# Places of a recurrence in the projections' memory, a memory projection in matmuls of 512 columns, and a preparation of two heads on one engine

## The chip, the cores and the metric

The kernel runs on one core of a Trainium2 chip. The metric is the device time of one execution in microseconds. The core has a matrix engine (TensorE, "PE" in the profile, with its weight loads as "PEld"), a vector engine (VectorE, "DVE"), a scalar engine (ScalarE, "ACT"), GpSimd ("POOL") and SyncE ("SP"), which in this kernel issues all DMAs. Each engine works through its own instructions in order and waits on semaphores for the others. Matmul results land in PSUM, eight banks of 128 rows by 512 fp32 values; all else lies in SBUF, 128 partitions wide.

## The reference, cut to what matters

One encoder layer on two sequences, 512 tokens (`x_sample`) and 256 tokens (`x_prompt`), 768 tokens in all, model width 1024. It has three parts: a mixer (an RWKV-7 recurrence beside a gated linear attention), a cross-attention to a memory of 256 rows per sequence, and a feed-forward layer.

```python
def rwkv7_scan(r, w, k, v, kk, a):
    def step(S, inp):
        r_t, w_t, k_t, v_t, kk_t, a_t = inp
        sa = jnp.einsum('bhij,bhj->bhi', S, -kk_t)
        S = (S * w_t[:, :, None, :] + sa[..., None] * (kk_t * a_t)[:, :, None, :]
             + v_t[..., None] * k_t[:, :, None, :])
        return S, jnp.einsum('bhij,bhj->bhi', S, r_t)
...
def hybrid_mixer(h, p):
    proj = h @ p['w_in']
    rw = centred_shift(proj[..., :R_COLS], p['mu_prev'], p['mu_next'])
    gl = proj[..., R_COLS:]
    mixed = jnp.concatenate([rwkv7_group(rw, p), gla_group(gl, p)], axis=-1)
    return mixed @ p['w_out']
...
def cross_attention(h, m, p):
    q = (h @ p['wq_x']).reshape(B, S, X_HEADS, X_HD)
    kv = (m @ p['wkv_x']).reshape(B, M, 2, X_HEADS, X_HD)
...
def encoder_trunk(x, mem, params):
        x = x + rms_norm(hybrid_mixer(rms_norm(x, p['g_mix_pre']), p), p['g_mix_post'])
        m = rms_norm(mem, p['g_mem'])
        x = x + rms_norm(cross_attention(rms_norm(x, p['g_x_pre']), m, p), p['g_x_post'])
        h = rms_norm(x, p['g_ffn_pre'])
        x = x + rms_norm(jnp.square(jax.nn.relu(h @ p['w_ff1'])) @ p['w_ff2'], p['g_ffn_post'])
```

The recurrence has 8 heads of 64 and runs once forwards and once backwards over each sequence. The gated linear attention (GLA) has 4 heads and is computed in chunks of 64 tokens, also in both directions.

## The kernel before, in words

All large products are split into a high and a low part (`split`, L143) and summed from three matmuls (`mm3`, L241). Weights are loaded as `wraw`, rounded by ScalarE to `whi` (L147), and the rest `wlo` is taken by GpSimd or VectorE (L148).

*Projections.* `hT_hi` and `hT_lo`, the normed input with its channels on the partitions, lie in pool `hp` on the right side of SBUF. Each block of 128 output channels is 24 matmuls of 512 columns and 24 of 256 (`channels_product`, L250). `gla_dense` (L468) makes the 16 blocks of the GLA and `rkv_early` (L446) the r, k, v blocks of a pair of heads; both write to DRAM through two tiles tagged `gd`. They are called through `blocks`, whose index is a GLA operand below 4 and a pair plus 3 from there on, so `(6, i)` are the three blocks of pair 3.

*Preparation of a pair* (`prep`, L692). The 8 heads of the recurrence are four pairs p, each with one head on partitions 0 to 63 and one on 64 to 127. For each direction d, `decays` makes the running product of decays, `bk_of` (L660) and `ar_of` (L669) form four products of 768 columns for each head, and `lower` (L678) makes the triangular part of 12 chunks of 64 tokens. In `bk_of` and `ar_of` VectorE works on the first head and GpSimd on the second, whose two operands lie in the opposite order. `invert` (L764) inverts the diagonal blocks of 32 by elimination on VectorE (L744, L746), and `joined` (L768) merges two blocks of 32 into one of 64 on TensorE (L788, L800). `begin` is `prep` plus a bonus term.

*The recurrence.* The chunks of a pair in both directions are grouped into 6 places g, each of 2560 columns. `products` (L973) loads a place's operands by six DMAs and computes what the steps use: 16 matmuls on 64 rows (L989 to L992) and 8 transposes (L1000). `step` (L1007) is one step of the recurrence: four groups of small matmuls (L1018, L1031, L1038, L1049) with ScalarE and VectorE in between. `stage(q)` (L1134) takes four steps, each for the second half of pair q-1 and the first and third part of pair q; there are stages 0 to 4. The places 0, 4, 1, 5, 2 lie in pool `mq1`, place 3 in `mq2`. The output of a pair goes to one of three tiles `ya`. `finish` (L1066) norms and gates it through a work tile `fb`.

*GLA heads.* `gla_head` (L825) works in an arena of 13 slots in pool `gp`: four slots alternate between even and odd heads, slots 8 to 12 are used by every head. Since `mq1` is opened when `gp` is closed, it lies on the arena's memory: no place can be loaded before the last head is done.

*Memory blocks.* `memory` (L1089) loads the two normed memories, 8 slices of 512 columns (256 for each sequence), into `mq2`, and `memory_block` (L1097) makes 16 blocks of keys and values from them, with 48 matmuls of 256 columns each (L1104). They stand between the steps of stages 1 to 3.

*Order.* A planner of the framework puts the instructions into the engines' queues. It takes them by a priority that is their order in the program, moved ahead by `high_priority(offset=...)` (steps by 4000, products by 3000, preparation and inversion by 2000 instructions), and by the times that its own model of the chip gives. A pool or a tag is reused when all that used the earlier tile is done. The program's order around the recurrence is: heads 0 to 3, preparations 1 and 2 and the blocks of L935 to L947; then products of pair 0, blocks `(6, i)`, stage 0, products for places 2 and 3, the loads of the memories, preparation 3, the join of pair 2, inversion 3, 16 memory blocks, stage 1, and so on. Behind the recurrence `w_out` is loaded into 32 planes of 512 columns, 20 of them on the places 0, 4, 1 and 5, and `out_projection` (L1251) follows, whose output `hh`, `hl` lies in a new pool on the right side.

Of the kernel before, what the change touches and what calls it, by code (L numbers as in the profile page):

```python
# [8 lines left out]
F32 = mybir.dt.float32  # L9
# [7 lines left out]
P = 128  # L17
D = 1024
# [14 lines left out]
def kernel(ctx: ExitStack, tc: tile.TileContext, I, y_prompt, y_sample):  # L33
# [30 lines left out]
    hp = hp_cm.__enter__()  # L64
    wp_cm = tc.tile_pool(name="wp", bufs=2, reuse_waits="tile")
# [380 lines left out]
    def rkv_early(p, i):  # L446

        ot = hp.tile([P, T], F32, tag="gd", bufs=2, name="gd")
# [8 lines left out]
    def tokens_first(ot):  # L457

        vt = hp.tile([P, T], F32, tag="gd", bufs=2, name="gd")
# [8 lines left out]
    def gla_dense(g, i):  # L468
# [3 lines left out]
        ot = hp.tile([P, T], F32, tag="gd", bufs=2, name="gd")  # L472
# [133 lines left out]
    tts, tdz = [], []  # L606
    for d in range(2):
        t = mp.tile([P, NCH, 64], F32, tag=f"tt{d}", name=f"tt{d}")
        pool.memset(t, 0.0)
        tts.append(t)  # L610
        tdz.append(mp.tile([P, NCH, 32], F32, name=f"tdz{d}"))
# [48 lines left out]
    def bk_of(pinv, nka, kd):  # L660

        b_ = pair_tile()
        dve.tensor_tensor(out=b_[0:64, :, 0, :], in0=v3(nka, 0, 64), in1=v3(pinv, 0, 64), op=ALU.mult)
        pool.tensor_tensor(out=b_[64:128, :, 1, :], in0=v3(nka, 64), in1=v3(pinv, 64), op=ALU.mult)
        dve.tensor_tensor(out=b_[0:64, :, 1, :], in0=v3(kd, 0, 64), in1=v3(pinv, 0, 64), op=ALU.mult)
        pool.tensor_tensor(out=b_[64:128, :, 0, :], in0=v3(kd, 64), in1=v3(pinv, 64), op=ALU.mult)
        return b_

    def ar_of(st, d):  # L669

        a_, kk, r_ = pair_tile(), st["kk"], st["r"]
        dve.tensor_tensor(out=a_[0:64, :, 0, :], in0=v3(kk, 0, 64), in1=px_prev[d][0:64], op=ALU.mult)
        pool.tensor_tensor(out=a_[64:128, :, 1, :], in0=v3(kk, 64), in1=px_prev[d][64:128], op=ALU.mult)
        pool.tensor_tensor(out=a_[64:128, :, 0, :], in0=v3(r_, 64), in1=px_at[64:128], op=ALU.mult)
        dve.tensor_tensor(out=a_[0:64, :, 1, :], in0=v3(r_, 0, 64), in1=px_at[0:64], op=ALU.mult)
        return a_

    def lower(st, d, b_, a_):  # L678

        lt = mp.tile([P, NCH, 64], F32, tag="lsb", bufs=4, name="lsb")  # L680
        for c0, n in ((0, 8), (8, 4)):
            pm = psn("low").rearrange("p (c x) -> p c x", x=64)
            for c in range(n):
                for h, hs in enumerate(HS):
                    pe.matmul(out=pm[hs, c, :], lhsT=b_[hs, c0 + c, h, :], rhs=a_[hs, c0 + c, h, :],
# [131 lines left out]
    with tc.tile_pool(name="gp", bufs=1, reuse_waits="tile") as gp:  # L817
# [134 lines left out]
    def open_places(pool_, gs):  # L952
        for g in gs:
            t = pool_.tile([P, 2560], F32, tag=f"pl{g}", name=f"pl{g}")
# [788 lines left out]
```

## Time and profile before

| | us |
|---|---|
| median of 3 runs | 1591.46 |
| lowest and highest of them | 1590.47, 1599.93 |
| the profiled execution | 1596.87 |
| its span, first to last instruction | 1595.0 |

The profile lists instructions with their line, engine, tiles and shapes. In a table of windows each row is a stretch of the span (start:end, length), then the busy time and the number of instructions of each engine, the TensorE clock that was granted (1.00 is full speed), the share of the DMA engines' time and the GB/s moved. In a timeline the columns are the start, the duration, engine, line, operation, tiles and shape, and in brackets the idle time before it and what ended that. In a list by line "x8: a/b/c" are the number of instructions and their shortest, median and longest duration in nanoseconds. Matmuls are pipelined: the distance between the starts of two says how long one holds the engine, its own duration says more than that.

Lines such as L247 or L148 belong to helpers that many parts of the kernel call; the tile names (`pd`, `wlo`, `bk`, `arena`) tell these parts apart.

### The profile page before, as it was taken

The numbers are of one execution on the slowest core, as the hardware profiler recorded it, in microseconds if no ns is written. First come the engines' busy times: TensorE is split into PE (matmuls) and PEld (weight loads), VectorE is DVE, ScalarE is ACT, GpSimd is POOL, SyncE is SP. The second block draws the span as 40 slices with busy tenths as digits, with TensorE's granted clock in tenths as the row PEclk, the third lists the DMA queues.
The fourth block names the chain that finished last, engine by engine and source line by source line (L and its number), as shares of the span: only waits on it lengthen the run. The fifth ranks groups of instructions, "written<-read, shape, count | busy, mean of one in ns | idle before, by whom it ended". The sixth has DMA issues, their size and how long they took to land. (4 is left out here: it accounts for less than half of the span.)

```text
span 1595.0 us, 28271 instructions
## 1 busy us (share of the span) xinstructions
PE 1442.8 (90%) x10614; PEld 1246.0 (78%) x10614; DVE 1049.7 (66%) x1605; ACT 718.9 (45%) x1417; POOL 514.6 (32%) x576
## 2 busy tenths in 40 slices
PE   7999689889887889899888999996999999999996
PEld 6887578777775777778767888786999999787785
DVE  5545885497577795764455434448876676878886
ACT  5754344443333332333344354434555556544442
POOL 6416643494317342211531354420000001231223
PEclk9999798989875988888979999997999999999998
DMA  6686555556468447754452333235555447564434
GB/s 168 181 302 188 167 137 131 145 146 192 111 205 229 127 149 176 205 134 135 126 166 99 119 95 105 73 111 160 172 169 176 158 145 284 171 204 132 143 100 142
DMA packets 279565, 250.35 MB, mean 157 GB/s; under 512 B 89264, under 2 KB 227059, under 8 KB 279428
## 3 DMA queue, kind: packets, MB, share of 16 engines
q1 hardware_dynamic: 279428, 248.54, 52.1%
q8 instruction: 84, 1.38, 0.4%
q14 instruction: 53, 0.43, 0.1%
HBM read 164.11 MB, written 82.58 MB: 155 GB/s over the span
## 5 line engine op out<-in xcount | busy, mean ns | idle before, releaser
L148 POOL TENSOR_TENSOR wlo<-wraw,whi 128x256 fp32r<-128x256 f32 x192 | 176.8, 934 | 331.0 <-ACT whi L147 231.1
L247 PE MATMUL pd<-hT_hi,whi 128*128 128x256 f32 (+1 forms) x512 | 182.0, 356 | 12.6 <-DVE gd L325 8.2
L247 PE MATMUL pd<-hT_hi,wlo 128*128 128x512 f32 (+1 forms) x512 | 180.1, 354 | 4.0 <-POOL wlo L148 4.0
L247 PE MATMUL pd<-hT_lo,whi 128*128 128x256 f32 (+1 forms) x512 | 178.6, 350 | 0.3 <-DVE hT_lo L206 0.3
L1511 POOL TENSOR_TENSOR wl<-w,wh 128x1024 fp32r<-128x1024 f32 x8 | 21.2, 2649 | 329.8 <-ACT wh L1510 329.8
L247 PEld LDWEIGHTS pd<-hT_hi,whi 128*128 128x128 f32 x512 | 100.4, 196 | 27.6 <-issue 5.5
L247 PEld LDWEIGHTS pd<-hT_hi,wlo 128*128 128x128 f32 x512 | 99.6, 195 | 18.6 <-POOL wlo L148 5.3
L147 ACT ACTIVATE whi<-wraw 128x256 fp32r<-128x256 f32 x192 | 77.3, 414 | 78.2 <-PE pd L1104 22.9
L247 PEld LDWEIGHTS pd<-hT_lo,whi 128*128 128x128 f32 x512 | 100.4, 196 | 13.0 <-DVE hT_lo L206 0.5
L148 DVE TENSOR_TENSOR ul<-ur,uh 128x768 fp32r<-128x768 f32 x56 | 77.4, 1388 | 30.7 <-ACT uh L147 17.7
L147 ACT ACTIVATE uh<-ur 128x768 fp32r<-128x768 f32 x56 | 47.4, 847 | 107.8 <-PE gz L1520 52.0
L1510 ACT ACTIVATE wh<-w 128x1024 fp32r<-128x1024 f32 x64 | 67.1, 1053 | 35.9 <-PE fz L1520 24.2
L1520 PE MATMUL gx<-wh,uh 128*128 128x512 f32 x192 | 75.0, 397 | 4.3 <-DVE acc L1713 4.3
L1511 DVE TENSOR_TENSOR wl<-w,wh 128x1024 fp32r<-128x1024 f32 x56 | 68.2, 1219 | 15.1 <-ACT wh L1510 14.5
L1520 PE MATMUL gx<-wl,uh 128*128 128x512 f32 x192 | 75.9, 395 | 0.0
L1520 PE MATMUL gx<-wh,ul 128*128 128x512 f32 x192 | 75.4, 395 | 0.0
L1520 PE MATMUL fz<-hh,wh 128*128 128x384 f32 x192 | 66.0, 344 | 1.9 <-ACT wh L1510 1.9
L1511 POOL TENSOR_TENSOR wl<-ws,wh 128x1024 fp32r<-128x1024 f32 x16 | 40.6, 2536 | 79.6 <-ACT wh L1510 79.6
L1520 PE MATMUL fz<-hh,wl 128*128 128x384 f32 x192 | 65.2, 344 | 0.8 <-DVE wl L1511 0.8
L1520 PE MATMUL fz<-hl,wh 128*128 128x384 f32 x192 | 65.8, 343 | 0.0
L1510 ACT ACTIVATE wh<-ws 128x1024 fp32r<-128x1024 f32 x48 | 50.5, 1052 | 26.8 <-PE fx L1520 22.3
L1104 PE MATMUL pd<-mem_hi,whi 128*128 128x256 f32 x256 | 59.3, 308 | 1.4 <-ACT mo L1116 1.4
(476 smaller groups left out, 4306.9 us busy)
## 6 DMA issues: line engine op xcount, KB each, us to landing
w<-in_w_ff_dram SPq DMA_DIRECT2D x64, 512.0 KB
ur<-ud SPq DMA_DIRECT2D x56, 384.0 KB
wraw<-in_w_in_dram SPq DMA_DIRECT2D x108, 128.0 KB
ud<-u SPq DMA_DIRECT2D x32, 384.0 KB
ud<-us SPq DMA_DIRECT2D x24, 384.0 KB
wraw<-in_wkv_x_dram SPq DMA_DIRECT2D x64, 128.0 KB
lora<-lo_t SPq DMA_DIRECT2D x20, 384.0 KB
bkg<-bkd SPq DMA_DIRECT2D x24, 256.0 KB
```

Of the source, the lines that this page charges most:

```text
L147: act.activation(out=hi, in_=src, func=AF.Copy)
L148: (lo_eng or pool).tensor_tensor(out=lo, in0=src, in1=hi, op=ALU.subtract)
L247: pe.matmul(out=out, lhsT=a, rhs=b, start=(i == 0), stop=(i == n - 1))
L1104: prev = order_after(pe.matmul(out=pd[:, c0:c0 + 256], lhsT=x, rhs=y[:, c0:c0 + 256], start=(k + i + c0 == 0), stop=(k + i + c0 == KD + 25 ...
L1510: act.activation(out=hi, in_=t[name], func=AF.Copy)
L1511: lo_eng.tensor_tensor(out=lo, in0=t[name], in1=hi, op=ALU.subtract)
L1520: pe.matmul(out=out, lhsT=a, rhs=b, start=first and i == 0, stop=last and i == n - 1, skip_group_check=True)
```

## The change

The places 0, 4, 1, 5 and 3 move into the memory of `hT_hi` and `hT_lo` (tags `hh` and `hl` of pool `hp`, which stays open), except for a part of place 3 that lies in `mq1` together with place 2. The tiles `gd` get a pool of their own, `gdp`; two of the tiles `ya` reuse them, the third reuses `kds`. `mq1` is opened on the right side. The pool `gp` of the GLA heads is closed later: heads 2 and 3, preparation 2 and inversion 2 now stand behind stage 0 and the products of places 2 and 3; the blocks `(6, i)` stand in front of them. `mq2`, with the memories, is opened after that. `finish` works in tag `sxf`, a tile of the inversions. 18 of the planes of `w_out` lie in a pool `wo1` that is opened on the left side.

A memory block is 24 matmuls of 512 columns, both memories at once. In `bk_of` and `ar_of` VectorE makes all four products on 128 partitions, with both heads in the same order; `products` turns the second head's order round where it loads the operands (two DMAs where one was) and where it transposes them (a transpose and a matmul with the identity where a transpose was).

```diff
@@ bk_of, ar_of, lower @@
-        dve.tensor_tensor(out=b_[0:64, :, 0, :], in0=v3(nka, 0, 64), in1=v3(pinv, 0, 64), op=ALU.mult)
-        pool.tensor_tensor(out=b_[64:128, :, 1, :], in0=v3(nka, 64), in1=v3(pinv, 64), op=ALU.mult)
-        dve.tensor_tensor(out=b_[0:64, :, 1, :], in0=v3(kd, 0, 64), in1=v3(pinv, 0, 64), op=ALU.mult)
-        pool.tensor_tensor(out=b_[64:128, :, 0, :], in0=v3(kd, 64), in1=v3(pinv, 64), op=ALU.mult)
+        dve.tensor_tensor(out=b_[:, :, 0, :], in0=v3(nka), in1=v3(pinv), op=ALU.mult)
+        dve.tensor_tensor(out=b_[:, :, 1, :], in0=v3(kd), in1=v3(pinv), op=ALU.mult)
...
+        dve.tensor_tensor(out=a_[:, :, 0, :], in0=v3(kk), in1=px_prev[d], op=ALU.mult)
+        dve.tensor_tensor(out=a_[:, :, 1, :], in0=v3(r_), in1=px_at, op=ALU.mult)
...
-                    pe.matmul(out=pm[hs, c, :], lhsT=b_[hs, c0 + c, h, :], rhs=a_[hs, c0 + c, h, :],
+                    pe.matmul(out=pm[hs, c, :], lhsT=b_[hs, c0 + c, 0, :], rhs=a_[hs, c0 + c, 0, :],
@@ order ahead of the recurrence @@
         blocks([(5, i) for i in range(3)])
-        gla_head(2)
         blocks([(3, 3), (2, 3)])
-        begin(2)
-        invert(2)
-        gla_head(3)
+        blocks([(6, i) for i in range(3)])
@@ places @@
-    mq1_cm = tc.tile_pool(name="mq1", bufs=1, reuse_waits="tile")
+    mq1_cm = tc.tile_pool(name="mq1", bufs=1, side="right", reuse_waits="tile")
     mq1 = mq1_cm.__enter__()
-    open_places(mq1, (0, 4, 1, 5, 2))
-    yas = [mq1.tile([P, T], F32, tag="ya0", name="ya0")]
+    plh, pll = (hp.tile([P, KD * T], F32, tag=n, name="pl_" + n) for n in ("hh", "hl"))
+    for t, gs in ((plh, (0, 4)), (pll, (1, 5))):
+        for i, g in enumerate(gs):
+            whole_place(g, t[:, 2560 * i:2560 * i + 2560])
+    place(3, plh[:, 5120:5632], pll[:, 5120:5888], mq1.tile([P, 512], F32, tag="pl3", name="pl3"), plh[:, 5632:6144],
+          pll[:, 5888:6144])
+    whole_place(2, mq1.tile([P, 2560], F32, tag="pl2", name="pl2"))
+    yas = [gdp.tile([P, T], F32, tag="gd", bufs=2, name=f"ya{i}") for i in range(2)]
@@ products @@
-        for h, hs in enumerate(HS):
-            dma(a_[hs, :, h:h + 2, :].rearrange("p u i x -> p u (i x)"), ard[p][hs, g])
+        dma(a_[HS[0], :, 0:2, :].rearrange("p u i x -> p u (i x)"), ard[p][HS[0], g])
+        for i in range(2):
+            dma(a_[HS[1], :, 2 - i, :], ard[p][HS[1], g, :, i * 64:i * 64 + 64])
...
-                pe.transpose(out=pt[:, u, :], in_=fl(b_[HS[h], u]), identity=ident[HS[h], HS[h]])
+                if h == 0:
+                    pe.transpose(out=pt[:, u, :], in_=fl(b_[HS[0], u]), identity=ident[HS[0], HS[0]])
+                else:
+                    pe.transpose(out=pt[HS[0], u, :], in_=b_[HS[1], u, 1, :], identity=ident[HS[1], HS[1]])
+                    pe.matmul(out=pt[HS[1], u, :], lhsT=b_[HS[1], u, 0, :], rhs=ident[HS[1], HS[1]], start=True, stop=True)
@@ finish @@
+    def finish_tile():
+        return mp.tile([P, D], F32, tag="sxf", name="fb")[:, 0:T]
...
-        pb, bon, gt = tiles or (mq2.tile([P, T], F32, tag="fb", name="fb"),) * 3
+        pb, bon, gt = tiles or (finish_tile(),) * 3
@@ memory_block @@
-        pd, prev = psd("pd"), None
-        for k, (wh, wl) in enumerate(w):
-            for i, (x, y) in enumerate(((wh, mem[k][0]), (wh, mem[k][1]), (wl, mem[k][0]))):
-                for c0 in (0, 256):
-                    prev = order_after(pe.matmul(
-                        out=pd[:, c0:c0 + 256], lhsT=x, rhs=y[:, c0:c0 + 256],
-                        start=(k + i + c0 == 0), stop=(k + i + c0 == KD + 257)), prev)
+        pd = psd("pd")
+        mm3(pd, list(zip(w, mem)))
@@ order of the recurrence @@
     prods(0, (0, 4, 1, 5))
-    blocks([(6, i) for i in range(3)])
     stage(0)
-    prods(0, (2,))
-    hp_cm.__exit__(None, None, None)
+    prods(0, (2, 3))
+    gla_head(2)
+    begin(2)
+    invert(2)
+    gla_head(3)
+    gp_cm.__exit__(None, None, None)
     mq2_cm = tc.tile_pool(name="mq2", bufs=1, reuse_waits="tile")
     mq2 = mq2_cm.__enter__()
-    open_places(mq2, (3,))
-    yas += [mq2.tile([P, T], F32, name=f"ya{i}") for i in (1, 2)]
-    prods(0, (3,))
     mem = memory()
     begin(3)
     joined(2)
     invert(3)
+    yas.append(mp.tile([P, T], F32, tag="kds", name="ya2"))
     for b in range(16):
         memory_block(mem, b)
+    mq2_cm.__exit__(None, None, None)
     stage(1)
@@ output weights @@
-    planes = []
+    wo1_cm = tc.tile_pool(name="wo1", bufs=1, reuse_waits="tile")
+    wo1 = wo1_cm.__enter__()
+    planes = [wo1.tile([P, 512], F32R, name=f"w_out{i}") for i in range(18)]
...
-    for g in (0, 4, 1, 5):
-        t = mq1.tile([P, 5, 512], F32R, tag=f"pl{g}", name=f"w_pl{g}")
-        planes += [t[:, i, :] for i in range(5)]
```

More of the change, by code (lines that the diff above doesn't have):

```diff
@@ L64 @@
     hp = hp_cm.__enter__()
+    gdp_cm = tc.tile_pool(name="gdp", bufs=1, side="right", reuse_waits="tile")
+    gdp = gdp_cm.__enter__()
     wp_cm = tc.tile_pool(name="wp", bufs=2, reuse_waits="tile")
@@ L446, in rkv_early @@
     def rkv_early(p, i):
-        ot = hp.tile([P, T], F32, tag="gd", bufs=2, name="gd")
+        ot = gdp.tile([P, T], F32, tag="gd", bufs=2, name="gd")
         rkv_block(p, i, lambda c, n: ot[:, c:c + n])
@@ L457, in tokens_first @@
     def tokens_first(ot):
-        vt = hp.tile([P, T], F32, tag="gd", bufs=2, name="gd")
+        vt = gdp.tile([P, T], F32, tag="gd", bufs=2, name="gd")
         for c, n in SEQS:
@@ L471, in gla_dense @@
         w = load_block([(w_cols(c0, P), 0)], P)
-        ot = hp.tile([P, T], F32, tag="gd", bufs=2, name="gd")
+        ot = gdp.tile([P, T], F32, tag="gd", bufs=2, name="gd")
         for c, n, pd in channels_product(w, P, hT_hi, hT_lo):
@@ L605 @@
     mp = mp_cm.__enter__()
-    tts, tdz = [], []
+    tdz = mp.tile([P, 2, NCH, 32], F32, tag="tdz", name="tdz")
+    tdz = [tdz[:, d] for d in range(2)]
+    tts = []
     for d in range(2):
@@ L814 @@
     joined(0)
-    with tc.tile_pool(name="gp", bufs=1, reuse_waits="tile") as gp:
+    gp_cm = tc.tile_pool(name="gp", bufs=1, reuse_waits="tile")
+    gp = gp_cm.__enter__()
+    if True:
         ones_f = gp.tile([P, P], F32, name="ones_f")
@@ L989, in products @@
             pe.matmul(out=sa[64:128, u, :], lhsT=b_[0:64, u, 1, :], rhs=fl(a_[0:64, u, 0:2, :]), start=True, stop=True)
-            pe.matmul(out=sb[0:64, u, :], lhsT=b_[64:128, u, 0, :], rhs=fl(a_[64:128, u, 1:3, :]), start=True, stop=True)
+            pe.matmul(out=sb[0:64, u, :], lhsT=b_[64:128, u, 1, :], rhs=fl(a_[64:128, u, 1:3, :]), start=True, stop=True)
             pe.matmul(out=sa[0:64, u, 64:128], lhsT=b_[0:64, u, 0, :], rhs=a_[0:64, u, 1, :], start=True, stop=True)
-            pe.matmul(out=sb[64:128, u, 0:64], lhsT=b_[64:128, u, 1, :], rhs=a_[64:128, u, 1, :], start=True, stop=True)
+            pe.matmul(out=sb[64:128, u, 0:64], lhsT=b_[64:128, u, 0, :], rhs=a_[64:128, u, 1, :], start=True, stop=True)
         dve.tensor_tensor(out=u2(a_[64:128, :, 0, :]), in0=u2(sa[64:128, :, 0:64]), in1=bc2(m_strict[64:128]), op=ALU.mult)
@@ L1186 @@
     mo = [mp.tile([P, T], F32, tag="lsb", bufs=4, name="mo") for _ in range(2)]
-    tiles = (mq2.tile([P, T], F32, tag="fb", name="fb"), *mo)
+    tiles = (finish_tile(), *mo)
     with tc.high_priority(offset=2000):
@@ L1192 @@
         finish(sts[3], SEQS[:1], tiles, mix[3])
-    mq2_cm.__exit__(None, None, None)
-    hp_cm = tc.tile_pool(name="hp2", bufs=1, side="right", reuse_waits="tile")
-    hp = hp_cm.__enter__()
     for k in order:
@@ L1202 @@
         planes += [t[:, 0, :], t[:, 1, :]]
-    for g in (0, 4, 1, 5):
-        t = mq1.tile([P, 5, 512], F32R, tag=f"pl{g}", name=f"w_pl{g}")
-        planes += [t[:, i, :] for i in range(5)]
+    planes.append(mp.tile([P, T], F32R, tag="tdz", name="w_tdz")[:, 0:512])
     planes += [mq1.tile([P, 512], F32R, tag="bkg", bufs=3, name="w_bkg") for _ in range(3)]
@@ L1208 @@
     planes += [t[:, i, :] for i in range(5)]
+    planes.append(mq1.tile([P, 512], F32R, tag="pl3", name="w_pl3"))
     wt = {}
```

25 lines of the change are left out of this document (10 added, 15 removed).

## The prediction

> **What bounds the kernel now.** I read the page first, then a table of busy time by stage, then the rows of the instructions that the change touches.
>
> ```profile
> span 1595.0 us, 28271 instructions
> PE 1442.8 (90%) x10614; PEld 1246.0 (78%) x10614; DVE 1049.7 (66%) x1605; ACT 718.9 (45%) x1417; POOL 514.6 (32%) x576
> ```
>
> TensorE is the engine to watch, but 90% is an average over unlike stages. I cut the span where the kinds of work change: projections, preparation and gated linear attention (GLA) heads to 442 us; then the recurrence, whose stages 0, 1, 2 and 3 fill the next four stretches and whose stage 4 opens the last.
>
> ```profile
> core 0: us, PE busy (x) PEld busy (x) DVE busy (x) ACT busy (x) POOL busy (x), PEclk, DMA share, GB/s
> 100.00:442.00 342.00, 298.11 (x2176) 252.31 (x2176) 234.68 (x298) 152.47 (x276) 174.81 (x172) 0.88 0.58 160
> 442.00:515.00 73.00, 56.51 (x748) 46.40 (x748) 56.98 (x102) 27.97 (x76) 35.81 (x31) 0.64 0.78 219
> 515.00:605.00 90.00, 77.12 (x962) 65.87 (x961) 74.95 (x158) 29.69 (x83) 37.78 (x32) 0.84 0.52 147
> 605.00:705.00 100.00, 90.08 (x1291) 77.69 (x1288) 68.32 (x182) 34.90 (x95) 18.68 (x25) 0.93 0.68 172
> 705.00:785.00 80.00, 78.14 (x1050) 66.83 (x1047) 33.61 (x92) 32.27 (x89) 18.53 (x29) 0.85 0.45 125
> 785.00:840.00 55.00, 44.17 (x274) 32.76 (x273) 28.95 (x64) 21.82 (x57) 22.90 (x36) 0.81 0.54 163
> ```
>
> Up to 442 us TensorE is busy 298 of 342 us: the stage is nearly bound by it, and work taken out of it shortens it. Stage 0 (442 to 515 us) is the opposite: 56.5 of 73 us busy at a granted clock of 0.64, so at full speed the same work is 0.64 x 56.5 = 36 us. Half of that stage is waiting. Stages 1 to 3 are filled by the memory blocks, and stage 2 takes 20 us longer than stage 3. The change moves work between just these stretches; before 100 us and behind 840 us it changes little.
>
> **The change part by part.**
>
> *Two heads leave the projections.* The places of five of the six groups go into the memory of the projections' input, so the recurrence can start when the last projection is done, and no longer when the last GLA head has freed its arena. Heads 2 and 3, and the preparation of pair 2, stand behind stage 0 in the program. What four heads cost (busy time of the instructions on the heads' arena; the three rows are TensorE, VectorE and ScalarE in turn):
>
> ```profile
> core 0: us, PE busy (x), PEclk, DMA share, GB/s
> 100.00:442.00 342.00, 62.93 (x472) 0.88 0.58 160
> ...
> 100.00:442.00 342.00, 75.52 (x52) 0.88 0.58 160
> ...
> 100.00:442.00 342.00, 73.64 (x100) 0.88 0.58 160
> ```
>
> Two of four heads are 31.5 us of TensorE, 37.8 of VectorE and 36.8 of ScalarE. If all of it leaves a TensorE-bound stage, the recurrence starts 31.5 us earlier; if the planner still runs them early (head 2's inputs are there), nothing is gained and nothing lost. I take 20, nearer the upper end because the stage is 87% busy.
>
> *What the heads cost in stage 0.* Their 31.5 us of TensorE lie beside 73 - 36 = 37 us that are free there at full speed. VectorE has 73 - 57 = 16 us free against 37.8, less what is run early. Also, the memory blocks' input now takes the arena's memory, so it is loaded only behind head 3. In the trace the first memory matmul stands 61 us behind the last projection, and GpSimd's share of the 16 input slices is 13.9 us:
>
> ```profile
> 442.24 0.28 PE L247 MATMUL pd<-hT_hi,wlo 128*128 128x256 f32 x1
> ...
> L1104 PE MATMUL pd<-mem_hi,whi x256: 274/281/581, 503.0 to 789.3; 128*128 128x256 f32 x128
> ...
> L148 POOL TENSOR_TENSOR mem_lo<-raw,mem_hi 128x256 fp32r<-128x256 f32 x16 | 13.9, 903 | 2.2 <-ACT mem_hi L147 2.1
> ```
>
> One head, run as a chain, is (62.93 + 75.52 + 73.64) / 4 = 53 us; head 3's inputs are ready three projection blocks earlier. It ends between 20 us (alone) and 75 us (behind the whole of head 2) after the last projection, and the 16 slices then need some 15 us more (an estimate, from the 13.9). So the memory blocks start between 26 us earlier and 29 us later than now. I take a loss of 6, the ends for the range.
>
> *Places wait for the last projection.* Now the first place is loaded while projections still run. The first such transfer is issued at 436.7 and the first product starts at 440.8:
>
> ```profile
> L41 SPq DMA_DIRECT2D pl<-ard x48: 573/602/2264, 436.7 to 768.6; - x48
> L989 PE MATMUL sca<-pl,bkg x192: 269/269/473, 440.8 to 773.0; 64*64 64x128 f32 x192
> ```
>
> That 4 us is hidden by projections and will be bare: a loss of 4 (0 if a head's matmuls fill it, 6 with the other places' transfers queued on SP).
>
> *Preparation on 128 partitions.* Per pair and direction four VectorE and four GpSimd products of 64 partitions become four VectorE products of 128.
>
> ```profile
> L672 DVE TENSOR_TENSOR bk<-kk,px x8: 1489/2428/2564, 153.0 to 594.6; 64x768 f32<-64x768 f32 x8
> L664 POOL TENSOR_TENSOR bk<-wb,wa x8: 1807/2203/2487, 150.0 to 590.1; 64x768 f32<-64x768 f32 x8
> L654 DVE TENSOR_TENSOR kds<-wc,k x4: 948/1472/2454, 157.7 to 558.9; 128x768 f32<-128x768 f32 x4
> L665 DVE TENSOR_TENSOR bk<-kds,wa x4: 951/1646/2548, 159.2 to 560.6; 64x768 f32<-64x768 f32 x4
> ...
> sum 1495.00, DVE 65.11; mean DVE 8.14
> ```
>
> The last row is the busy time of all 32 VectorE products of these tiles. A 64-row product takes 0.95 us at best and 2.4 at the median; a 128-row one (L654) 0.95 at best and 1.47 at the median. The time goes by elements along the row, not by partitions, and is stretched when GpSimd works beside it. So 32 new products cost 32 x 0.95 = 30 to 32 x 1.47 = 47 us in place of 65.1: VectorE gains 18 to 35 us, and GpSimd loses 32 instructions of about 2.2 us (70 us). I take 18 in all, the median. By the Trainium skill (SBUF — State Buffer, section "SBUF: two separate sides") a VectorE instruction with two SBUF inputs and a GpSimd instruction that reads SBUF exclude each other for their whole length; by that rule the 0.95 us holds whenever GpSimd rests and VectorE would gain 35. The trace agrees only in part: 0.95 and 1.81 one after the other would be 2.76, and the pair runs in 2.4.
>
> What of this is on the path? In pair 0 TensorE waited for exactly these:
>
> ```profile
> 181.44 1.97 PE L685 MATMUL low<-bk 64*64 64x64 f32 x32 [6.82 <-DVE bk L672]
> 188.32 0.77 PE L247 MATMUL pd<-hT_hi,whi 128*128 128x512 f32 x1 [4.91 <-DVE gd L325]
> ```
>
> 11.7 us idle there, the second one a projection's result queued on VectorE behind the products. For pairs 0 and 1 I take a gain of 8 (0 to 17), for pairs 2 and 3 a gain of 6 (0 to 17).
>
> *Inversion of pair 2 earlier.* Stage 2 needs its products, they its inversion, and that ran from 515 to 605 us between the steps of stage 1:
>
> ```profile
> 515.00:605.00 90.00, 12.79 (x29) 0.84 0.52 147
> ```
>
> (VectorE time of the inversion's line L744, of whose 31 instructions 29 stand in this stretch: 13 us of work drawn out over 90.) With preparation 2 shorter and VectorE freer in front of stage 0, it can end before stage 1 does. The prize is at most the 20 us by which stage 2 exceeds stage 3; heads 2 and 3 compete for the same engine, so it could also lose as much. I take a gain of 10.
>
> *Both memories in one matmul of 512.* 768 matmuls of 256 columns become 384 of 512.
>
> ```profile
> 660.02 0.40 PE L1104 MATMUL pd<-mem_hi,wlo 128*128 128x256 f32 x2
> 660.25 0.40 PE L1104 MATMUL pd<-mem_hi,whi 128*128 128x256 f32 x2
> 63.07 0.39 PE L247 MATMUL pd<-hT_lo,whi 128*128 128x512 f32 x1
> 63.30 0.39 PE L247 MATMUL pd<-hT_hi,wlo 128*128 128x512 f32 x1
> ```
>
> Starts are the measure: two of 256 take 0.23 us, one of 512 takes 0.23. TensorE gains nothing to 1.5 us. A step of the recurrence that is queued behind such a matmul waits up to 0.12 us longer; 48 steps of four matmul groups, half a difference each, half of them met: 6 us at most. I take a loss of 1.
>
> *Products.* For the second head a transpose onto 128 partitions becomes a transpose and an ordinary fp32 matmul, each onto 64. A matmul of that size is two records, so each of 24 products gets 8 more:
>
> ```profile
> 667.47 0.45 PE L1023 MATMUL rec<-pl 64*64 64x64 f32 x8
> 667.75 0.40 PE L1031 MATMUL rec<-rh,pl 64*64 64x64 f32 x8
> 485.61 0.69 PE L1023 MATMUL rec<-pl 64*64 64x64 f32 x8
> 486.09 0.64 PE L1031 MATMUL rec<-rh,pl 64*64 64x64 f32 x8
> ```
>
> Eight start within 0.28 us at full clock and 0.48 at half: 24 x 0.28 = 7 to 12 us of TensorE. I take a loss of 7; 0 if the two halves overlap. One DMA of a product becomes two of half its size: 24 more issues on SP of 0.60 us (the row above), 14 us spread over some 340; I cost them at nothing, since the transfers run a step ahead of the products, and at 2 if they do not.
>
> *The finish tile.* It moves onto a tile that the inversions use, so the finish of pair 0 must wait for the inversion of pair 3, and stage 3 writes the tile that this finish reads.
>
> ```profile
> L744 DVE TENSOR_TENSOR stmp<-sqf,snf x124: 192/388/1642, 209.0 to 691.3; 112x31 f32<-112x31 f32 x8, 112x60 f32<-112x60 f32 x8, 112x87 f32<-112x87 f32 x8, 112x112 f32<-112x112 f32 x8
> ...
> L800 PE MATMUL merge<-tt,sqf x384: 191/191/258, 282.9 to 729.9; 32*32 32x32 f32 x192
> ...
> L631 PE MATMUL hsum<-ya,ones_bd x16: 377/538/697, 631.9 to 831.9; 128*128 128x512 f32 x8, 128*128 128x256 f32 x8
> ...
> L1083 DVE TENSOR_TENSOR ya<-ya,fb x3: 942/959/1071, 662.2 to 797.9; 128x768 f32<-128x768 f32 x3
> ```
>
> Inversion 3 ends at 691 us, its join, on which stage 3 waits too, at 730; the first finish ran from 632 to 663, 31 us. The tie costs nothing as long as the join's 39 us cover it; without that cover stage 3 would start up to 31 us later.
>
> *Output weights.* 18 of their planes no longer wait for the recurrence's places. TensorE is short of work at two spots there:
>
> ```profile
> 800.00:810.00 10.00, 4.90 (x44) 2.95 (x42) 6.84 (x14) 5.03 (x14) 6.08 (x11) 0.50 0.58 181
> 840.00:850.00 10.00, 5.70 (x17) 4.23 (x18) 4.04 (x6) 2.66 (x7) 0.42 (x2) 0.83 0.09 26
> ```
>
> 9.4 us idle; the second spot is the finish itself. I take a gain of 4 (0 to 9).
>
> **Sum:** -20 + 6 + 4 - 8 - 6 - 10 + 1 + 7 - 4 = -30 us. The profiled execution took 1596.87 us; its span of 1595.0 would become 1565.0 and its time 1566.9. The median of the runs, 1591.46, lies 5.4 below the profiled time, so I predict 1561.5, rounded 1562.
>
> **The rivals.**
>
> *Stage 0 gives it back: no change.* The heads are sparse on TensorE, and a stage of waits runs at a low clock: 0.64 in stage 0 against 0.88 before it. At a clock of 0.5 the heads' 31.5 us become 31.5 x 0.88 / 0.5 = 55, so 24 us of the 30 are returned: 1562 + 24 = 1586. For it speaks that nothing dense is left for stage 0; against it, that stage 0 has 37 us free and the chain of steps, not TensorE, ends it. By the Trainium skill (TensorE: Matmul & The Clock Gate, section "What's actually happening") the throttled clock is the default and about 3.4 us of steady work releases it; by that rule this rival is the likelier one. The trace agrees on the two levels, and shows the low one through most of stage 0.
>
> *The memory blocks start late: slower.* Place: the first memory matmul behind head 3. If heads 2 and 3 run wholly one after the other behind the last projection, through their shared slots, head 3 ends 106 us after it and the first memory matmul comes 121 us after it, 60 later than now. Stages 1 to 3 are filled by these blocks, so they end 60 us later at worst; with the 6 us that the sum has for it taken out: 1562 + 54 = 1616. It decides, against the other 36 us of gain, once the blocks start more than 36 us later than now relative to the last projection. For it speaks VectorE's 16 free microseconds in stage 0; against it, VectorE's 107 free microseconds before 442 us, where head 2's inputs are ready.
>
> *More than the sum:* the upper ends of the heads, the preparation and the inversion together would add 11 + 9 + 10 = 30 us: 1532.
>
> **How the numbers follow.** 1562 or better has 0.62, no change 0.22, slower 0.16. Only over 1% can be told from no change, so 1576 and 1607 part the cases. The forecast's own range is 1532 to 1576. The range for 8 in 10 goes from 1530 to 1602: it takes in the larger gain and the no-change rival, and leaves out most of the slower one.
>
> **What would show it.** Right: the last projection before 425 us, the first memory matmul within 60 us of it, writes of the `bk` tiles near 1 us with none on GpSimd, inversion 2 done before stage 1, memory matmuls of 512 at 0.23 us each. Wrong: a stage 0 longer than 73 us at a clock of 0.6 (no change), or first memory matmuls over 95 us behind the last projection (slower), or stage 3 waiting for the finish of pair 0.

## The result, and the profile after

The changed kernel takes 1664.53 us (median of 4 runs, 1660.88 to 1669.26) against 1593.98 for the kernel before on the same chip: a ratio of 1.044, interval 1.0395 to 1.0485. It is 70 us slower; 1562 was forecast. The two head lines of its page, and busy time by stretch with the columns of the prediction's table:

```profile
span 1667.6 us, 27891 instructions
PE 1479.8 (89%) x10422; PEld 1245.5 (75%) x10422; DVE 1014.8 (61%) x1605; ACT 720.5 (43%) x1417; POOL 433.4 (26%) x544
```

```profile
100.00:412.00 312.00, 270.46 (x1922) 228.79 (x1920) 188.57 (x279) 123.61 (x233) 115.26 (x139) 0.88 0.64 175
412.00:515.00 103.00, 86.63 (x873) 64.71 (x874) 51.37 (x117) 22.42 (x59) 2.51 (x4) 0.55 0.57 154
515.00:607.00 92.00, 54.73 (x528) 45.37 (x525) 67.22 (x101) 33.72 (x52) 19.27 (x20) 0.56 0.42 110
607.00:680.00 73.00, 55.61 (x685) 42.58 (x681) 56.17 (x139) 27.54 (x78) 23.97 (x28) 0.71 0.41 102
680.00:860.00 180.00, 179.36 (x2119) 135.19 (x2119) 77.07 (x216) 74.69 (x206) 42.04 (x57) 0.98 0.45 131
```

TensorE is busy for 37 us more than before, and from 412 to 607 us it runs at little over half speed and is idle for 54 us as well; from 680 to 860 it is full at full speed, with everything that had not been done earlier. The recurrence alone (the same stretches of time, TensorE's time on the steps' tile `rec` and the number of its matmuls, then the clock, the DMA share and the GB/s):

```profile
412.00:505.00 93.00, 22.33 (x296) 0.56 0.59 162
505.00:607.00 102.00, 0.00 (x0) 0.55 0.42 107
607.00:640.00 33.00, 12.15 (x200) 0.66 0.33 91
640.00:860.00 220.00, 56.31 (x1248) 0.94 0.46 127
```

The first product starts at 412.75 us, 28 earlier than before; the forecast had 16, 20 from the projections less 4 of bare waiting. Then no step runs for 102 us. The next rows show the last projections, the heads (L854 on VectorE makes the last operand that a head's first matmuls, L863, need) and the memory matmuls, as a list by line. Behind it stand the first output projection, a row of the timeline, and the window in front of it.

```profile
L249 PE MATMUL pd<-hT_hi,wlo x144: 274/337/628, 301.7 to 409.6; 128*128 128x512 f32 x72, 128*128 128x256 f32 x72
...
L854 DVE TENSOR_TENSOR arena<-arena x2: 946/952/959, 297.3 to 556.3; 128x768 f32<-128x768 f32 x2
...
L863 PE MATMUL gs<-arena x96: 218/290/366, 526.1 to 576.8; 64*64 64x64 f32 x96
L914 PE MATMUL go<-arena x48: 342/474/532, 549.6 to 610.8; 128*128 128x64 f32 x48
L922 PE MATMUL gsum<-arena,ones_f x8: 531/848/1220, 570.9 to 617.0; 128*128 128x512 f32 x4, 128*128 128x256 f32 x4
...
L249 PE MATMUL pd<-mem_hi,whi x128: 389/396/801, 645.3 to 863.9; 128*128 128x512 f32 x128
```

```profile
890.86 1.19 PE L249 MATMUL po<-w_out,mix_bk 128*128 128x512 f32 x2 [16.92 <-ACT w_out L149]
```

```profile
860.00:890.80 30.80, 9.63 (x75) 5.80 (x73) 14.59 (x28) 11.10 (x26) 21.38 (x38) 0.73 0.62 185
```

The main part of heads 2 and 3 runs from 526 to 617 us, though head 2's operands were ready at 298.3. The first memory matmul stands 236 us behind the last projection (61 before), the last one at 864 (789 before), and only then come the output weights, for which TensorE waits 17 us. Before, the output projection's first matmul was at 808.4.

The preparation did what was said: its 32 products are all on VectorE, most at 0.95 us (three of the five groups).

```profile
L666 DVE TENSOR_TENSOR bk<-wb,wa x8: 945/956/1492, 152.0 to 559.2; 128x768 f32<-128x768 f32 x8
L673 DVE TENSOR_TENSOR bk<-kk,px x8: 946/952/1496, 153.4 to 560.1; 128x768 f32<-128x768 f32 x8
...
L667 DVE TENSOR_TENSOR bk<-wc,wa x4: 944/1126/2119, 182.3 to 563.3; 128x768 f32<-128x768 f32 x4
```

### The profile page after: what moved, and what is told of

Same layout as the page of the kernel before. It is cut to its first block, busy times and chain, and to the rows that moved or that the text cites. A ratio compares the mean times of both kernels' runs of the same rounds, so it can differ in the third digit from the quotient of the medians.

```text
span 1667.6 us, 27891 instructions
## 1 busy us (share of the span) xinstructions
PE 1479.8 (89%) x10422; PEld 1245.5 (75%) x10422; DVE 1014.8 (61%) x1605; ACT 720.5 (43%) x1417; POOL 433.4 (26%) x544
## 5 line engine op out<-in xcount | busy, mean ns | idle before, releaser
L150 POOL TENSOR_TENSOR wlo<-wraw,whi 128x256 fp32r<-128x256 f32 x192 | 164.5, 870 | 345.4 <-ACT whi L149 277.3
L249 PE MATMUL pd<-hT_hi,wlo 128*128 128x256 f32 (+1 forms) x512 | 180.7, 355 | 0.4 <-POOL wlo L150 0.3
L249 PEld LDWEIGHTS pd<-hT_lo,whi 128*128 128x128 f32 x512 | 101.0, 197 | 13.5 <-DVE hT_lo L208 0.5
L1530 PE MATMUL gz<-wl,uh 128*128 128x512 f32 x144 | 56.8, 395 | 0.0
```

What stands on the lines that cost most here:

```text
L150: (lo_eng or pool).tensor_tensor(out=lo, in0=src, in1=hi, op=ALU.subtract)
L249: pe.matmul(out=out, lhsT=a, rhs=b, start=(i == 0), stop=(i == n - 1))
L1530: pe.matmul(out=out, lhsT=a, rhs=b, start=first and i == 0, stop=last and i == n - 1, skip_group_check=True)
```

## The experiments

The theories: (1) heads 2 and 3 behind stage 0 hold up the memory blocks and the steps; (2) the products' new transposes cost far more than 7 us; (3) as rivals, the preparation, the memory matmuls or the places cost time by themselves. "The kernel before" stands at 1590.2 to 1594.0 us in these runs; ratios are to it, from runs on the same chip.

### One part of the change alone, in the kernel before

*Memory matmuls of 512.* The edit is the change's own in `memory_block`.

> The kernel before with only the memory blocks in matmuls of 512. Theory (the loss comes from where heads 2 and 3 stand): this part is neutral, 1586 to 1598 us, memory matmuls 0.23 us apart. Rival (the new parts themselves cost): slower by more than 1%, above 1607 us.

Measured: 1586.38 us, ratio 0.9970 (0.9953 to 0.9987): a small gain.

*Preparation on 128 partitions, with the products as changed* (`bk_of`, `ar_of`, `lower`, `products`).

> The kernel before with only the preparation on 128 partitions and the products that follow from it. Theory (the loss comes from where heads 2 and 3 stand): 1575 to 1594 us, the 32 products at about 0.9 us each, the later products some 7 us dearer on TensorE in all. Rival (the new parts themselves cost): slower by more than 1%, above 1607 us.

Measured: 1605.18 us, ratio 1.0084 (1.0066 to 1.0102): slower, where a gain was expected. The tile `bktp` took 62.7 us of TensorE, 25.1 before. The timeline of this variant, one product of the second head (L1000 the transpose, L1001 the matmul), and one of the kernel before:

```profile
445.75 0.31 PE L1000 MATMUL bktp<-ident,bkg 64*64 64x64 f32 x1
445.99 0.47 PE L1001 MATMUL bktp<-ident,bkg 64*64 64x64 f32 x2
446.39 0.31 PE L1000 MATMUL bktp<-ident,bkg 64*64 64x64 f32 x1
446.63 0.47 PE L1001 MATMUL bktp<-ident,bkg 64*64 64x64 f32 x2
...
448.31 0.69 PE L1050 MATMUL rec<-pl 128*64 128x64 f32 x8
```

```profile
444.02 0.46 PE L1000 MATMUL bktp<-ident,bkg 64*128 64x64 f32 x4
444.41 0.44 PE L1018 MATMUL rec<-pl 64*64 64x64 f32 x6
```

From one transpose to the next is 0.64 us, and the next instruction starts 2.56 us after the first of four; four plain transposes took 0.39 before. The clocks differ, 0.50 and 1.00 in these moments, but that is the smaller part: this variant's first product, at 438.27 us and still at full clock, took 0.43 us a pair, and four plain transposes at half clock take 0.62 (`c_grouped`, 478.29 us). And the stage grew cold (the stretch of stage 0 in this variant; before it was 56.51 busy at 0.64):

```profile
442.00:515.00 73.00, 69.22 (x714) 55.58 (x712) 34.10 (x86) 16.78 (x48) 0.70 (x3) 0.50 0.50 144
```

TensorE counts as busy for 95% of the stretch and is granted half its clock all the way. The clock fell from 1.00 to 0.50 between 440 and 441 us, right behind that first product; before, it stayed at 1.00 until 450. The Trainium skill (TensorE: Matmul & The Clock Gate, section "Part 4: PE-mode transpose") says that transposes do not count as activity for the clock gate as matmuls do. This row fits that, but the number of transposes alone does not decide: grouped (the next variant), the same transposes ran at 0.65 in this stretch.

*The same, transposes and matmuls grouped.*

```diff
                 else:
                     pe.transpose(out=pt[HS[0], u, :], in_=b_[HS[1], u, 1, :], identity=ident[HS[1], HS[1]])
-                    pe.matmul(out=pt[HS[1], u, :], lhsT=b_[HS[1], u, 0, :], rhs=ident[HS[1], HS[1]], start=True, stop=True)
+            for u in range(4 * h):
+                pe.matmul(out=pt[HS[1], u, :], lhsT=b_[HS[1], u, 0, :], rhs=ident[HS[1], HS[1]], start=True, stop=True)
```

> The kernel before with the preparation on 128 partitions and the change's transposes and matmuls, but the second head's four transposes stand together and its four matmuls behind them. If the change from one mode to the other costs the time: bktp falls from 62.7 us of TensorE to under 40 and the time from 1605.2 to 1580-1593 us. If the number of instructions costs it (records twice as many): bktp stays over 50 us and the time over 1600 us.

Measured: 1586.38 us, ratio 0.9949 (0.9927 to 0.9972); `bktp` 42.3 us, a little over the 40 expected. The same instructions in another order are 19 us faster. Of the 38 us of TensorE that the change adds to `bktp`, 20 are the alternation and 17 the additional work. One group at half clock, four transposes in 0.56 us and four matmuls (eight records) in 1.11, so 1.67 us where the alternation took 2.56:

```profile
481.21 0.63 PE L1000 MATMUL bktp<-ident,bkg 64*64 64x64 f32 x4
481.77 1.11 PE L1003 MATMUL bktp<-ident,bkg 64*64 64x64 f32 x8
```

*The same, the order turned round by the loads, with the eight plain transposes of before.*

```diff
-        dma(b_, bkd[p][:, g])
+        dma(b_[HS[0]], bkd[p][HS[0], g])
+        for i in range(2):
+            dma(b_[HS[1], :, 1 - i, :], bkd[p][HS[1], g, :, i, :])
```

> The kernel before with the preparation on 128 partitions, but the second head's order of b is turned round where it is loaded (two transfers of half the size for one), so that the products keep their eight plain transposes. Theory A (the alternating transposes and matmuls cost what the preparation gains): the 1605.2 us of the variant with alternation fall to 1572-1588 us, the bktp tiles take about 25 us of TensorE again. Rival B (the preparation itself gains nothing, because VectorE now carries the work that GpSimd had done beside it): 1592-1605 us whatever the transposes are. Rival C (24 more transfers queued on SP make the products late): bktp falls to 25 us but the time stays over 1598 us.

Measured: 1601.45 us, ratio 1.0052 (1.0033 to 1.0070). `bktp` was back at 24.7 us, the time was not: rival C. The list of waits from 420 to 530 us, and SP's queue in that variant:

```profile
PE sca L988 <- DMA pl<-ard: 14.4, 3, 11.7
```

```profile
455.37 6.96 SPq L41 DMA_DIRECT2D pl<-ard  x9
462.42 1.50 SPq L41 DMA_DIRECT2D pl<-ttd  x3
463.96 3.78 SPq L41 DMA_DIRECT2D pl<-vtd  x6
467.79 5.81 SPq L41 DMA_DIRECT2D bkg<-bkd  x9
473.69 3.89 SPq L41 DMA_DIRECT2D pl<-ard  x6
```

SP issues without a gap, 0.5 to 0.8 us each, and a product waits 11.7 us, up to 477.5, for its operands. In all there are 72 issues more than before, since a transfer of b is split in three and 24 of a come from the change; the expectation counted too few. They are not free where four places are loaded one after the other.

*The same, the order turned round by ScalarE when it empties PSUM* (plain transposes, seven transfers as in the change).

```diff
-                if h == 0:
...
-                    pe.matmul(out=pt[HS[1], u, :], lhsT=b_[HS[1], u, 0, :], rhs=ident[HS[1], HS[1]], start=True, stop=True)
-            act.activation(out=bkt[:, :, h, :], in_=pt, func=AF.Copy)
+                pe.transpose(out=pt[:, u, :], in_=fl(b_[HS[h], u]), identity=ident[HS[h], HS[h]])
+            for i in range(h + 1):
+                o, s = (HS[i], HS[1 - i]) if h else (slice(0, P),) * 2
+                act.activation(out=bkt[o, :, h, :], in_=pt[s], func=AF.Copy)
```

> The kernel before with the preparation on 128 partitions; the second head keeps the changed order in the products, eight plain transposes are made, and ScalarE turns the order round as it takes the result from PSUM, in two copies of 64 partitions for one of 128. SP has 24 more transfers, not 48. If the alternation of transposes and matmuls and the queue on SP are the two costs: 1575-1588 us, bktp near 25 us of TensorE, no wait of a product over 5 us for the places' transfers. If the preparation itself gains nothing: 1592-1605 us.

Measured: 1587.98 us, ratio 0.9976 (0.9957 to 0.9995); `bktp` 24.6 us, no wait for a place over 2.4 us. It sits at the upper end of what was expected: the preparation is worth about 4 us here, and the alternating products cost 17 (1605.2 less 1588.0).

### Do the parts add up?

Each with memory matmuls of 512 added.

> The kernel before with memory matmuls of 512 and the preparation on 128 partitions, its order turned round at the load. Theory A with the 5 us measured for the memory matmuls alone: 1567-1583 us, faster than both kernels. Rival B: 1587-1600 us.

> The same with memory matmuls of 512. If the 5 us measured for these add up with the other gain: 1570-1584 us, faster than both kernels. If the two don't add up, as they did not with the order turned round at the load (1608 us against 1601): 1585-1600 us.

> The kernel before with memory matmuls of 512, the preparation on 128 partitions, and the second head's four transposes together and its four matmuls behind them. If the gains of the two parts add up (1586.4 each alone): 1578-1584 us, no better than the variant in which ScalarE turns the order round (1578.0). If they don't: 1585-1595 us.

Measured: 1608.37 us (ratio 1.0091, 1.0069 to 1.0113) with the order turned by the loads, 1577.95 (0.9913, 0.9882 to 0.9943) with it turned by ScalarE, 1588.48 (0.9978, 0.9961 to 0.9994) grouped. The first lies above both of its ranges, the second in the range of gains that add up, the third in the range of gains that don't. With the 5 us of the memory matmuls added, the three variants become 7 us slower, 10 us faster and 2 us slower (medians). In the first TensorE still waits 11.2 us for one place's transfers; why the third gains nothing stays open. The second is the fastest kernel of the study, 13.5 us faster than the kernel before and 87 us faster than the change.

### The place of the heads

*The changed kernel with heads 2 and 3, preparation 2 and inversion 2 back where they were.*

```diff
         blocks([(5, i) for i in range(3)])
+        gla_head(2)
         blocks([(3, 3), (2, 3)])
+        begin(2)
+        invert(2)
+        gla_head(3)
         blocks([(6, i) for i in range(3)])
...
     prods(0, (2, 3))
-    gla_head(2)
-    begin(2)
-    invert(2)
-    gla_head(3)
```

> The changed kernel, with heads 2 and 3, preparation 2 and inversion 2 back in front of the last projection blocks in the program; places, pools, products and memory blocks stay changed. Theory (the place of the heads in the program makes the loss): the stretch of half clock from 500 to 620 us is gone, time 1575 to 1600 us. Rival (places in the projections' memory make the loss, since no place can be loaded before the last projection): above 1630 us.

Measured: 1630.77 us, ratio 1.0245 (1.0219 to 1.0272): 34 us of the 70 are the heads' place, the rest is still there. The theory's range is missed by 31 us. The rival's is just met, but not through its cause: with the same places and plain transposes the kernel takes 1582.7 us (`e_cross_early`, below). The memory blocks now began at 471 us and were used up by 709; what remained of the recurrence ran alone:

```profile
709.00:850.00 141.00, 109.21 (x1408) 83.19 (x1406) 68.42 (x189) 37.51 (x109) 12.91 (x24) 0.65 0.33 91
```

*The changed kernel, heads 2 and 3 on other banks of PSUM.* The heads share two tags of banks with the steps and the products.

```diff
         def gla_head(h):
+            hm, hc = (psm, psy) if h < 2 else (psd, psd)
```

(In the body `psm` and `psy` become `hm` and `hc`.)

> The changed kernel, with heads 2 and 3 in the PSUM banks of the projections (tag d) in place of those of products and steps (tags m and c). Theory (heads behind stage 0 and stage 1 wait for each other's PSUM banks): stage 1 starts before 560 us in place of 608, time 1600 to 1635 us. Rival (the heads' own chain and the arena that the memories wait for are enough): first memory matmul still near 645 us, time 1655 to 1670.

Measured: 1637.75 us, ratio 1.0282 (1.0261 to 1.0303), between the two ranges, with the memory blocks still starting at 637.8. The steps' row for the stretch that was empty, and the heads' first matmuls (L865 in this variant):

```profile
505.00:607.00 102.00, 31.10 (x512) 0.67 0.37 95
```

```profile
L865 PE MATMUL gs<-arena x96: 216/290/366, 411.5 to 529.5; 64*64 64x64 f32 x96
```

512 matmuls of steps in place of none: it was the banks that stopped the recurrence, and that is worth 27 us of the 70. The banks had held up head 2 as well: it now starts at 411.5 us, 7 behind the last projection, where it had started at 526.1. Yet head 3's last matmul is at 611.3, 6 us earlier than in the change. What draws the two heads out over 200 us here was not found.

*The kernel before, memory blocks made late.* The memory tiles wait for an output of stage 1; no head is moved.

```diff
         res = [(hi[:, k, :], lo[:, k, :]) for k in range(KD)]
+        dve.tensor_copy(out=hi[:, :, 0], in_=yas[1][:, 200:208])
...
-    mem = memory()
     begin(3)
     joined(2)
     invert(3)
+    stage(1)
+    mem = memory()
     for b in range(16):
         memory_block(mem, b)
-    stage(1)
```

> The kernel before, where the memories' tiles wait for the outputs of stage 1, so that the memory blocks start at about 620 us instead of 503; the heads stay where they are. In the kernel before 48.5 us of memory matmuls lie in stages 0 and 1 up to 605 us. If a late start of the memory blocks alone costs time, as the slower rival has it: 1620-1645 us (48.5 us less the up to 20 us by which a stage 1 without them is shorter). If the later stages have room for them: 1592-1605 us, and then what slows the changed kernel is the heads' hold on PSUM and the clock, not the late memory.

Measured: 1620.47 us, ratio 1.0181 (1.0145 to 1.0217), the low end of what the rival of late memory blocks expected. The first memory matmul is at 594.6 us, 92 later than before, and stage 1 lost its filling (before: 77.12 busy at 0.84):

```profile
515.00:605.00 90.00, 61.69 (x788) 48.93 (x782) 80.56 (x181) 23.84 (x71) 29.18 (x21) 0.59 0.45 112
```

A late start alone costs 29 us, with no head and no bank in the way.

### Heads and products together

The changed kernel with plain transposes, turned by the loads (`d_swap`) and by ScalarE (`h_cross`); the latter with the heads early (`e_cross_early`); the old preparation with the heads late and early (`h_late_noprep`, `h_places`).

> The changed kernel with the second head's order turned round at the load and its plain transposes back; all else of the change stays. If the products' alternation is a part of the 70 us that adds up with the rest: 1640-1650 us (the 14 to 25 us that it costs in the kernel before). If it is hidden behind the heads that keep TensorE waiting from 500 to 620 us: 1658-1668 us. If it caused the heads' lateness: under 1620 us.

> The changed kernel with heads 2 and 3, preparation 2 and inversion 2 back in front of the last blocks of projections, and with plain transposes, whose order ScalarE turns round. If the heads' place and the alternation are separate costs that add up: 1630.8 less 14 to 20 = 1610-1617 us. If stages 3 and 4, which ran without memory blocks beside them in the kernel with the heads early, set the end whatever the products cost: 1625-1632 us.

> The changed kernel whole, heads 2 and 3 behind stage 0, with plain transposes whose order ScalarE turns round. Beside the same with the heads early (1582.7) it gives the price of the heads' place. If that price is the 34 us measured with the alternation: 1612-1622 us. If the two add up from the changed kernel's side as the 17 us of the turning at the load did: 1640-1650 us, and the heads' place costs some 60 us once nothing else is in the way.

> The changed kernel with the preparation and the products of the kernel before; places, memory matmuls of 512 and the order of the heads stay as changed. If the heads' place costs by itself: 1630-1655 us. If it costs only together with the new preparation and its products: under 1605 us.

> The same with heads 2 and 3, preparation 2 and inversion 2 back in front of the last projections: of the change only the places in the projections' memory, the memory matmuls of 512, the finish tile and the output weights are left. If these add nothing to the 5 us of the memory matmuls: 1580-1592 us. If the output weights and the earlier loads bring what was predicted (4 us and more): 1570-1580 us. If the tie of the finish tile or the earlier end of the memory blocks costs: 1595-1625 us.

Measured: 1647.54 us (ratio 1.0345, 1.0321 to 1.0368); 1582.65 (0.9944, 0.9921 to 0.9967), far better than the sum of the parts; 1625.26 (1.0212, 1.0181 to 1.0244); 1674.43 (1.0520, 1.0489 to 1.0550); 1594.92 (1.0022, 1.0006 to 1.0039). Only the first lies in one of its ranges (costs that add up). The second is 27 us below both, the third 3 us and the fourth 19 us above the range of a price of the heads' place, and the last falls between two ranges. In a table (medians in us; the two lower rows have memory matmuls of 512 and the moved places):

| | products and preparation as before | 128 partitions, alternating | 128 partitions, turned by ScalarE |
|---|---|---|---|
| order and places as before | 1591.7; 1586.4 with 512 | 1605.2 | 1588.0; 1578.0 with 512 |
| places moved, heads early | 1594.9 | 1630.8 | 1582.7 |
| places moved, heads late | 1674.4 | 1664.5, the change | 1625.3 |

Down the columns the heads' place costs 80, 34 and 43 us: it costs by itself, whatever the products are. Preparation 2 and inversion 2 moved with the heads in every run, so this is the price of the three together. Along the rows the alternation costs 17, 48 and 39 us (second column less third). And the places, with the output weights and the finish tile, gain nothing: 1594.9 against 1586.4, and 1582.7 against 1578.0. One way through the table adds up: 1664.5 less 39 (alternation), less 43 (heads' place), less 5 (places) is 1578, the fastest kernel. With the heads early the last projection stands at 434 to 459 us, not at 410, so nothing starts earlier.

*What of the heads' 43 us is what.* The `h_cross` kernel with the heads on the other banks.

> The changed kernel with plain transposes (1625.3 us), and heads 2 and 3 take their PSUM banks from those of the projections and memory blocks (tag d) instead of sharing those of the recurrence and the products. With the heads early it was 1582.7 us. If the 43 us between them are the recurrence's steps waiting for banks that the heads hold: 1583-1600 us. If they are the late memory blocks, which still wait for the arena: 1610-1625 us, first memory matmul still over 150 us behind the last projection.

Measured: 1611.06 us, ratio 1.0134 (1.0092 to 1.0176), the steps running (377 of their matmuls from 505 to 607 us) and the first memory matmul at 607.0. Of 43 us some 14 are the banks and some 28 are left with the memory blocks late; the interval is 7 us to either side. That these 28 are the late blocks is not shown here: it rests on the like size of the 29 in `g_late`.

*Memory blocks spread.* In `e_cross_early`, 8 of the 16 blocks behind stage 1 in the program.

```diff
-    for b in range(16):
+    for b in range(8):
         memory_block(mem, b)
-    mq2_cm.__exit__(None, None, None)
     stage(1)
+    for b in range(8, 16):
+        memory_block(mem, b)
+    mq2_cm.__exit__(None, None, None)
```

> The kernel with heads early and plain transposes (1582.7 us), with 8 of the 16 memory blocks put behind stage 1 in the order of the program. There the memory blocks began at 469.5 us and were used up by 750. If stages 3 and 4 lack work beside the steps: 1566-1577 us. If the chain of steps sets the end of these stages whatever lies beside them: 1578-1590 us. If stages 0 and 1 are then short of work: over 1590 us.

Measured: 1582.18 us, ratio 0.9937 (0.9916 to 0.9959), no difference. The first memory matmul stayed at 470.6 and the last moved only from 750.0 to 740.1, so the edit hardly changed what it was meant to change, and it settles nothing on stages 3 and 4.

## Why the prediction was wrong

*Two heads leave the projections (-20):* right, even at its upper end. The last projection moved from 442.2 to 409.6 us. It was worth nothing, since what it freed was lost behind it.

*What the heads cost in stage 0 (+6): the step that failed.* "It ends between 20 us and 75 us after the last projection": head 3's last matmul is at 617.0, 207 us after it. I counted the heads' engine time and the free time in stage 0, and took for granted that the heads run as soon as their inputs are ready. Head 2's operands were ready at 298.3, but its first matmuls stand at 526.1, behind stage 0. From there the two heads took 91 us, not 106: the chain was sized well, its start was not. And I priced TensorE, VectorE and ScalarE, but not the PSUM banks that heads and steps share: 102 us without a step, 27 us of time with the alternating products, about 14 with plain ones. With banks of its own head 2 starts at 411.5 (`a_heads_d`), so the banks, and not only the planner's order, kept it back in stage 0.

*The slower rival* is the one that came true, in its place (first memory matmul behind head 3) and beyond its size (236 us behind the last projection, 121 forecast). Its price of one us for each us of delay was too high: `g_late` has 29 us for 92. It carried a chance of 0.16 because VectorE had free time before 442 us "where head 2's inputs are ready"; free time of an engine did not bring the head forward. The rival of a cold stage 0 holds as a description (clock 0.55 from 412 to 515 us, 103 us long).

*Products (+7): mis-sized.* The variant in the kernel before shows 17 us of time and 38 us of TensorE. The row that I took, eight records in 0.28 to 0.48 us, is of matmuls for two heads on two halves of the array, which overlap. These eight all have the same half, and take 1.11 us as a group; alternating with transposes they take longer still. In the changed kernel they cost 39 us of time, and 48 with the heads early. TensorE's additional time on `bktp` is nearly the same each time: 38 us in the kernel before, 41 with the heads early, 39 in the change. Why it reaches the end in full there and less than half of it in the kernel before was not settled.

*One DMA more, at nothing or 2:* right for the 24 issues of the change (2.4 us of waits in `e_cross`), no rule for more: with 72, turned by the loads, the kernel is 13.5 us slower than with 24 (1601.45 against 1587.98).

*Preparation (-14):* mis-sized, and for the most part not on the path. The 32 products fell from 65.1 us of VectorE to 36.0, a gain of 29 where 18 was taken and 35 was the upper bound; all of VectorE fell by 34.9 (1049.7 to 1014.8). With no GpSimd product beside them, all groups but one have a median under 0.97 us, so the 1.47 of L654 was the wrong row to go by. The prediction held against the lower price that a pair of 0.95 and 1.81 us ran in 2.4, and read this as an exclusion that holds only in part. The rows of the kernel before say more:

```profile
152.19 2.43 POOL L673 TENSOR_TENSOR bk<-kk,px 64x768 f32<-64x768 f32 x1
154.57 2.41 POOL L674 TENSOR_TENSOR bk<-r,px 64x768 f32<-64x768 f32 x1
```

```profile
152.96 2.46 DVE L672 TENSOR_TENSOR bk<-kk,px 64x768 f32<-64x768 f32 x1
155.35 2.44 DVE L675 TENSOR_TENSOR bk<-r,px 64x768 f32<-64x768 f32 x1
```

They end in turn, at 154.62 (GpSimd), 155.42 (VectorE), 156.98 and 157.79: a VectorE product 0.80 us behind a GpSimd one, a GpSimd one 1.56 behind a VectorE one. The two take turns, and the 2.4 us are the two turns; what is missing to 2.76 is some 0.2 us of each instruction that overlaps. By the Trainium skill's rule (SBUF — State Buffer, "SBUF: two separate sides") a GpSimd instruction that reads SBUF and a VectorE instruction with two SBUF inputs exclude each other. The trace agrees, up to these 0.2 us.

Only 4 us of the gain reached the end in the kernel before, 8 with the memory matmuls of 512. With the heads late the old preparation and the new are 49 us apart (1674.4 and 1625.3), but 31 of these are there at the last projection already (434.3 and 403.6 us), ahead of pair 2's preparation. How much of the rest that preparation brings was not tried.

*Inversion of pair 2 (-10):* in the changed kernel it ran from 500 to 600 us, before stage 1's first step at 607.8, as asked; but stage 1 itself was late. No run had it alone.

*Memory matmuls (+1):* the starts are 0.23 us apart, as read; the time gained 5 us. *First place waits (+4):* the first product waited 1.6 us. *Output weights (-4):* they became a wait of 17 us behind the late memory blocks; with the heads early (`e_cross_early`) TensorE was no busier from 785 to 840 us, 44.4 us against 44.2 before. *Finish tile (0):* not tried alone; all that is left with the heads early and the old preparation costs 8.5 us (1594.9 against 1586.4), and the tie could be a part of it. So could the last projection, which stands 18 us later there (458.9 us against 440.8 in `b_mem512`), and the two tiles `tdz`, which the change makes into one; none of these was tried alone.

## What to carry to other kernels

When work is moved behind another stage, list not only the engine time that it finds there but every slot that it shares with that stage (PSUM banks, tags) and every later tile that lies on its memory; the fill work that starts behind it kept the clock up here (0.84 in stage 1 with the memory blocks, 0.59 without). Inputs that are ready early do not make a planner run the work early: where the start matters, bound the case in which it comes last. When one matrix-engine instruction is split into two of different kinds, put like beside like (1586.4 us in place of 1605.2), and let another engine do the rearranging where it copies the result anyway.

## What was not expected of the hardware

Alternating transposes and fp32 matmuls on one half of the array took 0.64 us for each pair at half clock and 0.43 at full, 2.56 us for four pairs where groups of four and four took 1.67 (half clock). TensorE could count as busy for 69.2 of 73 us while its granted clock stayed at 0.50: busy time alone did not raise the clock here. ScalarE copied from PSUM to the other 64 partitions at its usual pace, so an exchange of halves cost one additional copy of 0.38 us for each product (`e_cross`).
